# Unit 8 of the third down pass in half-size products, residual rows summed by accumulating transfers, and the first attention's pool reused tile by tile

## The chip, the cores and the metric

The kernel runs on one core of a Trainium2 chip. The metric is device time in microseconds (us) of one launch. One execution is profiled, and all views below are of that execution.

## The reference, cut to what matters

One encoder block over 512 tokens of width 2048, all in fp32: an adaLN modulation, a combined input projection, a global grouped-query attention with normed and rotated q and k, a neighbourhood attention, a gated merge with an output projection and residual, and a SwiGLU feed-forward of inner width 5632 with residual, then a final RMS norm.

```python
qa = apply_rope(rms_norm(qa, q_norm_w[l]), cos, sin)
ka = apply_rope(rms_norm(ka, k_norm_w[l]), cos, sin)
ya = global_gqa(qa, ka, va)
...
merged = sigmoid(ga) * (ya @ w_oa[l]) + sigmoid(gb) * (yb @ w_ob[l])
x = x + g1 * (merged @ w_out[l])
h2 = rms_norm(x, norm2_w[l]) * (1.0 + sc2) + sh2
ff = (silu(h2 @ w_ffn_gate[l]) * (h2 @ w_ffn_up[l])) @ w_ffn_down[l]
x = x + g2 * ff
return rms_norm(x, final_w)
```

## The kernel before, in words

**Products.** An fp32 operand is kept as two tensors of the fast fp32r type, high and low. `split` makes them: ScalarE (ACT) writes the high part (L168), VectorE (DVE) subtracts it for the low part (L170). Each product is three matmuls, high by high, high by low and low by high (`mm3`, L188, L189, L190). Weights stream from HBM through `unit` (L195, SyncE's queue, 512 KB a piece, the tile `raw`) and are split into the tiles `whl`.

**Half-size products.** Many of the large products are done by seven products of half-size blocks in place of eight (a Strassen-Winograd form, indices r = 1 to 7). `wforms` makes the four sums of a weight's blocks (tiles `ta` and `tb`, L696 to L699) and splits them; `sforms` does the same for the activations (four sums of 512 columns, then three splits of 1024 and one of 512 columns). A unit of the down projection done so takes 84 matmuls of 256 columns, a plain unit 96.

**The stages** follow each other: modulation and input projection, the first attention, gates and values, the second attention, the merge and the output projection (which writes the new residual rows x2 to DRAM), gate and up, and then the down projection. Its inner width of 5632 is cut into 11 units of 512 (0 to 10), and the output width into four column groups cc = 0 to 3. The first pass takes units 0 and 1 for all cc, the second pass units 2 to 5, the third pass units 6 to 9, and the last stretch unit 10 with gate2 multiplied into its weights. Each pass loads its sums (`acc<-accd`) and stores them again.

**The third pass** is a loop over cc with `down_group`. For cc = 0 units 8 and 9 come first and plain, then 6 and 7 by half-size products; for cc = 1 to 3, 6 and 7 first and then 8 and 9 plain (`tail`). Behind each unit `late(cc)` issues what is due: at u = 7 the gated sum of the cc before (`gated_sum`: DVE multiplies the sums by gate2 and adds the residual rows `xr`, the result is stored as `x2pd`, and 1 MB of residual rows for the next cc is loaded); behind cc = 1's units 8 and 9 the activations of unit 10 (`fl`); behind cc = 3's unit 7 the load of gate2 over all rows (`gf<-g2d`), which the weights of unit 10 are multiplied by (`gated_split`, L1528); and behind cc = 3's unit 9 the weights of unit 10 and the loads of x2.

**Tiles.** The slots 0 to 2 (`s0...`, `s1...`, `s2...`) hold the activations' forms of units 2 to 4 in the second pass and of units 6 and 7 (slots 0 and 1) in the third; slot 2 holds `xr` and `fl` there. The areas `a0` and `a1` hold the pairs of plain units (`a1` those of unit 8) and later the last weights `w2` and `w3`.

**The first attention.** The pool `p_a` is allocated on the memory that the projection's pool `p_x` leaves. Without `reuse_waits="tile"` the first write to any tile of it waits for all that was done on that memory, with it for the work on that tile's own bytes. Before the attention, 12 tiles of gate sums are stored (`sga<-g_acc`). Then the rotation's table `rp` is loaded (L792, SyncE's queue), and `norm_rope` makes rotated heads on DVE (L811 norm, L812 cosine, L814 sine, L815 sum, tile `rt`), which TensorE transposes (L818, `T<-ident,rt`) among matmuls of the gates' projections.

**What sets the order.** A scheduler places the instructions in each engine's queue; `issue_after`, `behind` and `keep_in_program_order` pin some. Each engine works its queue in order, so an instruction that waits holds all behind it.

Of the kernel before, what the change touches and what calls it, by code (L numbers as in the profile page):

```python
# [20 lines left out]
P = 128  # L21
# [91 lines left out]
def encoder_block(ctx: ExitStack, tc, xp, xT, c, ada1_w, ada2_w, b_ada, norm1_w, w_in, q_norm_w, k_norm_w, bias,  # L113
# [476 lines left out]
    for k1 in range(1, KT + 1):  # L590
# [41 lines left out]
        if k1 < KT:  # L632
            ada1(k1)
    for j in range(12):
        nc.sync.dma_start(sg_a[j], g_acc[j])
# [155 lines left out]
    p_a = tc.alloc_tile_pool(name="p_a", bufs=1, side="right")  # L791
    behind(nc.sync.dma_start(rp, rope.rearrange("p (i s d) -> p i s d", i=NT, s=2)))  # L792
# [372 lines left out]
    x2_d = dram.tile([T, D], F32, name="x2d")  # L1165
# [19 lines left out]
    def residual(cc, g, ssq, eng, x, keep=None):  # L1185
        cs = slice(cc * 512, (cc + 1) * 512)

        def evac(i, b):
# [5 lines left out]
            if keep is not None:  # L1194
                t0 = i // 2 * 256 + i % 2
                nc.sync.dma_start(keep[t0:t0 + 255:2, cs], x(i, cc))
# [187 lines left out]
    def sforms(j, u):  # L1384

        big, low = slots[j]
        e, o = (raw_tile("ffe") for _ in range(2))
        for a, r in enumerate((e, o)):
            nc.gpsimd.dma_start(r, ff_d[u][:, a * 1024:(a + 1) * 1024])
        sa = wq.tile([P, 1024], F32, tag="ta", name="sa", bufs=2)  # L1390
        sb = wq.tile([P, 1024], F32, tag="tb", name="sb", bufs=1)
# [126 lines left out]
    xr = p_e.tile([P, 3072 + 64], F32, tag="s23072", name="xr")  # L1518
    xo = [xr[:, :2048].rearrange("p (i n) -> p i n", i=NT)]
    fl = p_e.tile([P, 4096 + 64], F32R, tag="s24096", name="fl")  # L1520
    wl = {}
    x2p_d = [dram.tile([P, NT, 512], F32, name=f"x2pd{cc}") for cc in range(3)]
# [9 lines left out]
    def late(cc):  # L1532
        def behind(u):
            if cc == 0 and u == 8:
                while bg:
                    pump()
            if cc == 1 and u > 7:
                a = u - 8
                xl_pairs.append(ff_pair(10, a, [fl[:, a * 2048 + e * 1024:a * 2048 + (e + 1) * 1024] for e in range(2)],
                                        pin=tc.keep_in_program_order))  # L1540
            if u == 7 and due:
                due.pop()()
# [4 lines left out]
            if cc == 3 and u == 7:  # L1547
# [3 lines left out]
                rows(wide2[0], g2_d)  # L1551
            if cc == 3 and u == 9:
# [3 lines left out]
                for c in range(3):  # L1556
                    nc.gpsimd.dma_start(x2[c], x2p_d[c])
# [7 lines left out]
    def factor(cc):  # L1565
        return xr[:, 2048 + cc % 2 * 512:2560 + cc % 2 * 512]

    def residual_of(cc):
        nc.gpsimd.dma_start(xo[0], x2_d[:, cc * 512:(cc + 1) * 512].rearrange("(i p) d -> p i d", p=P))
# [105 lines left out]
```

## Time and profile before

| | |
|---|---|
| time of 3 runs | 2459.8, 2462.04 (median), 2468.41 us |
| the profiled execution | 2466.89 us, span 2465.1 us, mean granted clock 0.998 |
| TensorE (PE) busy | 2433.0 us, 99% |
| VectorE (DVE) busy | 2007.1 us, 81% |
| ScalarE (ACT) busy | 1069.2 us, 43% |
| GpSimd (POOL) busy | 150.8 us, 6% |

The span is the time from the first to the last instruction in the trace; the profiled execution's own time is 1.8 us longer. Matmuls overlap in the pipeline, so that a busy TensorE is read by the distance from one matmul's start to the next; an engine's row ends with what ended the idle time ahead of it.

### The profile page before, as it was taken

What the parts mean: (1) busy time and instruction counts of PE and PEld (TensorE: products, weight loads), DVE (VectorE), ACT (ScalarE), POOL (GpSimd) and SP (SyncE); (2) the same over time, 40 slices, a digit from 0 to 9 for tenths busy, and PEclk for the clock granted to TensorE, in tenths of its full rate; (3) what the DMA queues carried; (4) which work ended last, traced back from release to release, by engine and by line L of the source; (5) the groups of instructions that cost most, each with busy time, mean ns of one, the idle gap of its engine ahead of it and who ended that gap; (6) DMA issues with size and microseconds to landing.
All of it is one profiled execution on the core that took longest, in us unless ns stands there. A gap on an engine that the chain in (4) does not pass through costs nothing.

```text
span 2465.1 us, 42367 instructions
## 1 busy us (share of the span) xinstructions
PE 2433.0 (99%) x17327; PEld 2279.4 (92%) x17327; DVE 2007.1 (81%) x2704; ACT 1069.2 (43%) x1466; POOL 150.8 (6%) x255
## 2 busy tenths in 40 slices
PE   8999999999999999999999999999999999999998
PEld 7888888999888888888999999999999998999997
DVE  7995778998677678667899889889899885687877
ACT  5223545544344523337744444444444454433333
POOL 0000000000011111111000000000000000000010
PEclk9999999999999999999999999999999999999999
DMA  9775232455767687867444454444454456546563
GB/s 354 291 261 159 82 98 83 146 180 187 245 206 235 214 297 248 301 204 230 137 154 154 140 163 153 127 156 154 138 171 139 136 189 223 187 155 231 192 246 126
DMA packets 213731, 461.77 MB, mean 187 GB/s; under 512 B 15153, under 2 KB 59553, under 8 KB 204833
## 3 DMA queue, kind: packets, MB, share of 16 engines
q1 hardware_dynamic: 174160, 309.76, 38.6%
q0 software_dynamic: 29872, 132.73, 15.8%
q10 hardware_dynamic: 9504, 16.58, 1.9%
q8 instruction: 136, 2.23, 0.4%
q14 instruction: 59, 0.48, 0.1%
HBM read 412.84 MB, written 46.17 MB: 186 GB/s over the span
## 4 chain that ended last, share of the span: by engine, by line
PE 71%; DVE 14%; issue 8%; DMA 5%; ACT 1%; POOL 0%; DVEq 0%; SPq 0%; POOLq 0%; ACTq 0%
PE mm L190 14%; PE mm L188 14%; PE mm L189 14%; PE S L188 6%; PE S L190 6%; PE S L189 6%; DVE whl L170 3%; PE Y L188 3%; PE Y L189 3%; PE Y L190 2%; DVE raw L524 2%; DMA raw<-in_w_down 2%; PE T L886 1%; DVE g_acc L631 1%; DMA raw<-in_w_in 1%
## 5 line engine op out<-in xcount | busy, mean ns | idle before, releaser
L168 ACT ACTIVATE whl<-raw 128x1024 fp32r<-128x1024 f32 (+1 forms) x483 | 453.7, 943 | 673.9 <-PE mm L190 292.2
L170 DVE TENSOR_TENSOR whl<-raw,whl 128x1024 fp32r<-128x1024 f32 (+1 forms) x483 | 517.5, 1086 | 124.0 <-ACT whl L168 123.7
L168 ACT ACTIVATE whl<-ta 128x1024 fp32r<-128x1024 f32 x124 | 131.4, 1060 | 182.6 <-PE mm L190 112.9
L168 ACT ACTIVATE whl<-tb 128x1024 fp32r<-128x1024 f32 x124 | 131.4, 1060 | 171.7 <-PE S L190 116.5
L170 DVE TENSOR_TENSOR whl<-ta,whl 128x1024 fp32r<-128x1024 f32 x124 | 151.3, 1220 | 41.8 <-ACT whl L168 41.5
L388 DVE SCALAR_TENSOR_TENSOR acc<-mw,cact,acc 128x1024 f32<-128x1024 f32 x124 | 158.8, 1281 | 19.6 <-DMA mw<-in_ada_w 19.3
L170 DVE TENSOR_TENSOR whl<-tb,whl 128x1024 fp32r<-128x1024 f32 x124 | 150.9, 1217 | 5.9 <-ACT whl L168 5.8
L366 POOL DMA_DIRECT2D mw<-in_ada_w x113 | 60.3, 534 | 1357.1 <-DVE acc L388 939.2
L697 DVE TENSOR_TENSOR ta<-raw,ta 128x512 f32<-128x512 f32 x124 | 85.2, 687 | 65.4 <-DMA raw<-in_w_down 27.2
L696 DVE TENSOR_TENSOR ta<-raw 128x512 f32<-128x512 f32 x124 | 85.3, 688 | 36.3 <-DMA raw<-in_w_down 33.8
L188 PE MATMUL mm<-x56h,whl 128*128 128x256 f32 x336 | 92.7, 276 | 0.3 <-DVE c L784 0.2
L189 PE MATMUL mm<-x56l,whl 128*128 128x256 f32 x336 | 92.4, 275 | 0.0
L190 PE MATMUL mm<-x56h,whl 128*128 128x256 f32 x336 | 92.4, 275 | 0.0
L188 PE MATMUL mm<-x3h,whl 128*128 128x256 f32 x320 | 88.1, 275 | 0.5 <-DVE c L782 0.5
L188 PE MATMUL mm<-whl,s 128*128 128x256 f32 x320 | 88.2, 276 | 0.0
L189 PE MATMUL mm<-whl,s 128*128 128x256 f32 x320 | 88.1, 275 | 0.0
L190 PE MATMUL mm<-x3h,whl 128*128 128x256 f32 x320 | 88.0, 275 | 0.0
L190 PE MATMUL mm<-whl,s 128*128 128x256 f32 x320 | 88.0, 275 | 0.0
L189 PE MATMUL mm<-x3l,whl 128*128 128x256 f32 x320 | 88.0, 275 | 0.0
L190 PE MATMUL S<-x56h,whl 128*128 128x256 f32 x320 | 88.0, 275 | 0.0
L188 PE MATMUL S<-x56h,whl 128*128 128x256 f32 x320 | 88.0, 275 | 0.0
L189 PE MATMUL S<-x56l,whl 128*128 128x256 f32 x320 | 88.0, 275 | 0.0
(1879 smaller groups left out, 8909.2 us busy)
## 6 DMA issues: line engine op xcount, KB each, us to landing
raw<-in_w_in SPq DMA_DIRECT2D x133, 512.0 KB, 4.7
mw<-in_ada_w POOLq DMA_DIRECT2D x113, 512.0 KB, 4.5
raw<-in_w_gate SPq DMA_DIRECT2D x92, 512.0 KB, 4.6
raw<-in_w_up SPq DMA_DIRECT2D x88, 512.0 KB, 4.6
raw<-in_w_down SPq DMA_DIRECT2D x88, 512.0 KB, 5.3
raw<-in_ada_w POOLq DMA_DIRECT2D x29, 1024.0 KB, 5.3
raw<-in_w_out SPq DMA_DIRECT2D x48, 512.0 KB, 5.4
ffd<-c SPq DMA_DIRECT2D x10, 1024.0 KB, 4.8
```

The costliest lines, as they stand in the source:

```text
L168: high = pin(S.activation(hi, src, AF.Copy))
L170: latest[:] = [high, pin(eng.tensor_sub(lo, src, hi))]
L188: nc.tensor.matmul(o, lh, rh, start=start, stop=False, **kw)
L189: nc.tensor.matmul(o, lh, rl, start=False, stop=False, **kw)
L190: nc.tensor.matmul(o, ll, rh, start=False, stop=stop, **kw)
L366: mod["queue"].dma_start(w, ada2_w[n * P:(n + 1) * P, :])
L388: behind(V.scalar_tensor_tensor(acc, part, cact[:, k:k + 1], acc, op0=ALU.mult, op1=ALU.add))
L524: V.scalar_tensor_tensor(raw, raw, 1.0, call, op0=ALU.mult, op1=ALU.mult, accum_out=y)
L631: V.tensor_add(acc, acc, b)
L696: V.tensor_sub(t1, b12, b11)
L697: V.tensor_sub(t2_, b22, t1)
L886: nc.tensor.transpose(tp[:, k * P:(k + 1) * P], e[:, k * P:(k + 1) * P], ident)
```

## The change

**First attention.** `p_a` gets `reuse_waits="tile"`, and the load of `rp` is issued behind step k1 = 14 of the projection's loop, ahead of the stores of the gate sums.

**Third pass.** For cc = 1 to 3 unit 8 is done by half-size products, as 6 and 7 (`ss` is 6, 7, 8, the tail 9). Its activations' forms are made during cc = 0: one load of 1 MB (`f8`, in area `a1`, POOL's queue) behind unit 9, then four DVE sums and four splits into slot 2. `xr` goes from slot 2, `fl` to `a1` with its loads on SyncE's queue, `w2` to slot 2, `w3` to `a0`.

**Residual rows.** x2 lies in DRAM as eight tiles of 256 by 512. `gated_sum` only multiplies, and for cc = 0 to 2 a transfer from POOL's queue adds the product to x2 in DRAM (`accum_op=add`). For cc = 3 the residual rows are loaded behind unit 7, the DVE adds them; and cc = 2's gated sum moves from u = 7 to u = 8 in cc = 3.

```diff
@@ -631,6 +631,8 @@
                     V.tensor_add(acc, acc, b)
         if k1 < KT:
             ada1(k1)
+        if k1 == 14:
+            behind(nc.sync.dma_start(rp, rope.rearrange("p (i s d) -> p i s d", i=NT, s=2)))
     for j in range(12):
         nc.sync.dma_start(sg_a[j], g_acc[j])
     p_x.release()
@@ -788,8 +790,7 @@
                 V.tensor_add(d12, p[3], d12)
 
 
-    p_a = tc.alloc_tile_pool(name="p_a", bufs=1, side="right")
-    behind(nc.sync.dma_start(rp, rope.rearrange("p (i s d) -> p i s d", i=NT, s=2)))
+    p_a = tc.alloc_tile_pool(name="p_a", bufs=1, side="right", reuse_waits="tile")
     nw = {}
     for nm, w in (("q", q_norm_w), ("k", k_norm_w)):
         nw[nm] = small.tile([P, HD], F32, tag=f"nw{nm}", name=f"nw{nm}", bufs=1)
@@ -1162,7 +1163,7 @@
     more_buffers(1, 2)
     wq = tc.alloc_tile_pool(name="wq", bufs=1, side="right", reuse_waits="tile")
 
-    x2_d = dram.tile([T, D], F32, name="x2d")
+    x2_d = [[dram.tile([256, 512], F32, name=f"x2d{cc}{t}") for t in range(2)] for cc in range(4)]
     mod["queue"] = nc.sync
     p_r = tc.alloc_tile_pool(name="p_r", bufs=1, side="right", reuse_waits="tile")
     gate = p_r.tile([P, D], F32, name="gate1")
@@ -1192,8 +1193,7 @@
             if ssq:
                 square(x(i, cc), ssq[i][:, cc:cc + 1])
             if keep is not None:
-                t0 = i // 2 * 256 + i % 2
-                nc.sync.dma_start(keep[t0:t0 + 255:2, cs], x(i, cc))
+                nc.sync.dma_start(keep[cc][i // 2][i % 2::2, :], x(i, cc))
         return evac
 
     def w_out_pass(cc, tiles):
@@ -1381,14 +1381,19 @@
                 self.pairs[j] = ff_pair(self.u0 + n, a, place(self.at + n, a, self.off))
             return tuple(Tokens(half(t)[:, :, q]) for t in self.pairs[j])
 
-    def sforms(j, u):
+    def sforms(j, u, room=None):
 
         big, low = slots[j]
-        e, o = (raw_tile("ffe") for _ in range(2))
-        for a, r in enumerate((e, o)):
-            nc.gpsimd.dma_start(r, ff_d[u][:, a * 1024:(a + 1) * 1024])
-        sa = wq.tile([P, 1024], F32, tag="ta", name="sa", bufs=2)
-        sb = wq.tile([P, 1024], F32, tag="tb", name="sb", bufs=1)
+        if room is None:
+            e, o = (raw_tile("ffe") for _ in range(2))
+            for a, r in enumerate((e, o)):
+                nc.gpsimd.dma_start(r, ff_d[u][:, a * 1024:(a + 1) * 1024])
+            sa = wq.tile([P, 1024], F32, tag="ta", name="sa", bufs=2)
+            sb = wq.tile([P, 1024], F32, tag="tb", name="sb", bufs=1)
+        else:
+            e, o, sa, sb = (room[:, n * 1024:(n + 1) * 1024] for n in range(4))
+            nc.gpsimd.dma_start(room[:, :2048], ff_d[u])
+            yield
         a11, a21, a12, a22 = e[:, :512], e[:, 512:], o[:, :512], o[:, 512:]
         V.tensor_add(sa[:, :512], a21, a22)
         V.tensor_sub(sa[:, 512:], sa[:, :512], a11)
@@ -1515,11 +1520,13 @@
         nc.gpsimd.dma_start(acc_d[cc], acc)
 
     f0 = 40
-    xr = p_e.tile([P, 3072 + 64], F32, tag="s23072", name="xr")
-    xo = [xr[:, :2048].rearrange("p (i n) -> p i n", i=NT)]
-    fl = p_e.tile([P, 4096 + 64], F32R, tag="s24096", name="fl")
-    wl = {}
-    x2p_d = [dram.tile([P, NT, 512], F32, name=f"x2pd{cc}") for cc in range(3)]
+    fl, wl = [], {}
+    x2_of = lambda cc, t: x2_d[cc][t].rearrange("(i p) d -> p i d", p=P)
+
+    def load_x2(to, cc):
+        for t in range(2):
+            nc.gpsimd.dma_start(to[:, 2 * t:2 * t + 2], x2_of(cc, t))
+
     sq3 = [small.tile([P, 4], F32, tag=f"sq{i}", name=f"sq3{i}", bufs=1) for i in range(NT)]
 
     def gated_split(k, cc, hi, lo):
@@ -1534,12 +1541,16 @@
             if cc == 0 and u == 8:
                 while bg:
                     pump()
+            if cc == 0 and u == 9:
+                forms = sforms(2, 8, p_s.tile([P, 4096 + 64], F32, tag="a1", name="f8"))
+                next(forms)
+                bg.append(forms)
             if cc == 1 and u > 7:
                 a = u - 8
-                xl_pairs.append(ff_pair(10, a, [fl[:, a * 2048 + e * 1024:a * 2048 + (e + 1) * 1024] for e in range(2)],
-                                        pin=tc.keep_in_program_order))
-            if u == 7 and due:
-                due.pop()()
+                if a == 0:
+                    fl.append(p_s.tile([P, 4096 + 64], F32R, tag="a1", name="fl"))
+                xl_pairs.append(ff_pair(10, a, [fl[0][:, a * 2048 + e * 1024:a * 2048 + (e + 1) * 1024] for e in range(2)],
+                                        nc.sync, pin=tc.keep_in_program_order))
             if cc == 3 and u == 6:
                 xa = p_s.tile([P, 2, NT, 512], F32, tag="s04096", name="xa")
                 xb = p_s.tile([P, NT, 512], F32, tag="s03072", name="xb")
@@ -1549,12 +1560,15 @@
                 gf = p_s.tile([P, 2, D], F32, tag="s14096", name="gf")
                 wide2.extend((gf[:, 0], gf[:, 1]))
                 rows(wide2[0], g2_d)
+                load_x2(x2[3], 3)
+            if u == (8 if cc == 3 else 7) and due:
+                due.pop()()
             if cc == 3 and u == 9:
                 for c in range(2):
                     us = [gated_split(k, c, *wtiles()) for k in range(0, 4, 2)]
                     wl[c] = [tuple(t[:, e * 512:(e + 1) * 512] for t in hl) for hl in us for e in range(2)]
                 for c in range(3):
-                    nc.gpsimd.dma_start(x2[c], x2p_d[c])
+                    load_x2(x2[c], c)
                 nc.scalar.dma_start(wide2[1], final_w.partition_broadcast(P))
         return behind
 
@@ -1562,28 +1576,29 @@
     cl = {8: ahead[8], 9: {a: ff_pair(9, a, place(0, a, 0)) for a in range(2)}}
     due = []
 
-    def factor(cc):
-        return xr[:, 2048 + cc % 2 * 512:2560 + cc % 2 * 512]
-
-    def residual_of(cc):
-        nc.gpsimd.dma_start(xo[0], x2_d[:, cc * 512:(cc + 1) * 512].rearrange("(i p) d -> p i d", p=P))
-        nc.gpsimd.dma_start(factor(cc), g2_d[cc].partition_broadcast(P).rearrange("p o d -> p (o d)"))
+    def factor_of(cc):
+        f = p_e.tile([P, 512], F32, tag="g2f", name="g2f", bufs=2)
+        nc.gpsimd.dma_start(f, g2_d[cc].partition_broadcast(P).rearrange("p o d -> p (o d)"))
+        factors.append(f)
 
     def gated_sum(cc, acc):
-        to = xo[0] if cc < 3 else x2[3]
+        f = factors.pop(0).unsqueeze(1).to_broadcast([P, 2, 512])
         for t in range(2):
             ts = slice(2 * t, 2 * t + 2)
-            behind(V.tensor_mul(acc[:, ts], acc[:, ts], factor(cc).unsqueeze(1).to_broadcast([P, 2, 512])))
-            behind(V.tensor_add(to[:, ts], xo[0][:, ts], acc[:, ts]))
+            behind(V.tensor_mul(acc[:, ts], acc[:, ts], f))
+            if cc == 3:
+                behind(V.tensor_add(x2[3][:, ts], x2[3][:, ts], acc[:, ts]))
+            else:
+                nc.gpsimd.dma_start(x2_of(cc, t), acc[:, ts], accum_op=ALU.add)
         if cc < 3:
-            nc.gpsimd.dma_start(x2p_d[cc], xo[0])
-            residual_of(cc + 1)
-
-    residual_of(0)
+            factor_of(cc + 1)
+
+    factors = []
+    factor_of(0)
     for cc in range(4):
         acc = acc_tile()
         nc.gpsimd.dma_start(acc, acc_d[cc])
-        down_group(cc, (6, 7), cl, acc, late(cc), () if cc else (8, 9), late=cc > 1,
+        down_group(cc, (6, 7, 8) if cc else (6, 7), {9: cl[9]} if cc else cl, acc, late(cc), () if cc else (8, 9), late=cc > 1,
                    after_lead=cc == 1)
         due.append(functools.partial(gated_sum, cc, acc))
     due.pop()()
@@ -1591,7 +1606,7 @@
     g2, fw = wide2
     xs = [tuple(Tokens(half(t)[:, :, q]) for t in xl_pairs[a]) for a in range(2) for q in range(2)]
     for cc in range(2, 4):
-        wt = p_s.tile([P, 4096 + 64], F32R, tag=f"a{3 - cc}", name=f"w{cc}")
+        wt = (p_e if cc == 2 else p_s).tile([P, 4096 + 64], F32R, tag="s24096" if cc == 2 else "a0", name=f"w{cc}")
         hi, lo = (wt[:, 48 + e * 2048:48 + (e + 1) * 2048] for e in range(2))
         for k in range(0, 4, 2):
             sl = slice(k * 512, (k + 2) * 512)
```

The order of instructions on three places follows (a name is out<-in by the program's tiles, then the shape; x2 or x3 is a run of like rows).

**VectorE at the start of the first attention.** Names as above; `st` holds k's projection, `nwk` the norm's weight, `kl` the low part of the transposed k. Before:

```order
L170 TENSOR_TENSOR whl<-raw,whl 128x1024
L811 SCALAR_TENSOR_TENSOR rt<-st,rr,nwk 128x128 x2
L170 TENSOR_TENSOR whl<-raw,whl 128x1024
L812 TENSOR_TENSOR rt<-rt,rp 128x256
L814 TENSOR_TENSOR rt<-rt,rp 128x128 x2
L815 TENSOR_TENSOR rt<-rt 128x256
L811 SCALAR_TENSOR_TENSOR rt<-st,rr,nwk 128x128 x2
L812 TENSOR_TENSOR rt<-rt,rp 128x256
L170 TENSOR_TENSOR kl<-T,kh 128x2x128
```

Of the change (the lines are one further down):

```order
L170 TENSOR_TENSOR whl<-raw,whl 128x1024
L812 SCALAR_TENSOR_TENSOR rt<-st,rr,nwk 128x128 x2
L813 TENSOR_TENSOR rt<-rt,rp 128x256
L815 TENSOR_TENSOR rt<-rt,rp 128x128 x2
L816 TENSOR_TENSOR rt<-rt 128x256
L812 SCALAR_TENSOR_TENSOR rt<-st,rr,nwk 128x128 x2
L813 TENSOR_TENSOR rt<-rt,rp 128x256
L815 TENSOR_TENSOR rt<-rt,rp 128x128 x2
L170 TENSOR_TENSOR kl<-T,kh 128x2x128
```

The weight's split that stood between the norm (L811, now L812) and the cosine (L812, now L813) now stands behind this stretch.

**VectorE in the third pass, cc = 0, from the weight sums of unit 6 on.** `s_21037` and `s_21038` are slot 2's tiles, `f_23713` is `f8`; `whl` are split weights of units 6 and 7. Before:

```order
L697 TENSOR_TENSOR ta<-raw,ta 128x512
L170 TENSOR_TENSOR whl<-tb,whl 128x1024
L698 TENSOR_TENSOR tb<-raw 128x512
L699 TENSOR_TENSOR tb<-raw,ta 128x512
L1468 TENSOR_TENSOR acc<-acc,S 128x2x256
L170 TENSOR_TENSOR whl<-raw,whl 128x512
L170 TENSOR_TENSOR whl<-raw,whl 128x1024
L170 TENSOR_TENSOR whl<-ta,whl 128x1024
```

Of the change:

```order
L699 TENSOR_TENSOR ta<-raw,ta 128x512
L1398 TENSOR_TENSOR f_23713<-f_23713 128x512
L1400 TENSOR_TENSOR f_23713<-f_23713 128x512
L1399 TENSOR_TENSOR f_23713<-f_23713 128x512
L170 TENSOR_TENSOR s_21037<-f_23713,s_21037 128x1024
L170 TENSOR_TENSOR whl<-tb,whl 128x1024
L1401 TENSOR_TENSOR f_23713<-f_23713 128x512
L170 TENSOR_TENSOR s_21037<-f_23713,s_21037 128x512
L700 TENSOR_TENSOR tb<-raw 128x512
L170 TENSOR_TENSOR s_21038<-f_23713,s_21038 128x1024
L1473 TENSOR_TENSOR acc<-acc,S 128x2x256
L701 TENSOR_TENSOR tb<-raw,ta 128x512
```

Unit 8's four sums (L1398 to L1401) and four splits now stand ahead of or among the splits that unit 6 and unit 7 need, three of the sums and one split ahead of `whl<-tb` of unit 6.

**VectorE in the third pass, cc = 3, around unit 9's weights.** The rows `whl<-raw` are unit 9's splits and then unit 10's; L1528 (now L1535) multiplies unit 10's weights by `gf`; the rows of `acc` with `p`, `mm`, `q`, `v` gather the half-size products. Before:

```order
L1577 TENSOR_TENSOR xr<-xr,acc 128x1024
L170 TENSOR_TENSOR whl<-raw,whl 128x1024 x2
L1472 TENSOR_TENSOR acc<-acc,mm 128x2x256
L1473 TENSOR_TENSOR acc<-acc,mm 128x2x256
L1474 TENSOR_TENSOR q<-S,p 128x512
L170 TENSOR_TENSOR whl<-raw,whl 128x1024
L1475 TENSOR_TENSOR acc<-acc,q 128x2x256
L1476 TENSOR_TENSOR v<-S,q 128x512
L170 TENSOR_TENSOR whl<-raw,whl 128x1024
L1479 TENSOR_TENSOR acc<-acc,v 128x2x256
L1480 TENSOR_TENSOR acc<-acc,v 128x2x256
L1528 TENSOR_TENSOR raw<-raw,gf 128x1024 x3
```

Of the change:

```order
L170 TENSOR_TENSOR whl<-tb,whl 128x1024
L1588 TENSOR_TENSOR acc<-acc,g2f 128x1024 x2
L1535 TENSOR_TENSOR raw<-raw,gf 128x1024
L1476 TENSOR_TENSOR acc<-acc,p 128x2x256
L170 TENSOR_TENSOR whl<-raw,whl 128x1024 x3
L1477 TENSOR_TENSOR acc<-acc,mm 128x2x256
L1478 TENSOR_TENSOR acc<-acc,mm 128x2x256
L1479 TENSOR_TENSOR q<-S,p 128x512
L1535 TENSOR_TENSOR raw<-raw,gf 128x1024
L1480 TENSOR_TENSOR acc<-acc,q 128x2x256
L1481 TENSOR_TENSOR v<-S,q 128x512
```

Before, the four splits of `raw` into `whl` (of units 8 and 9) were ahead of the first product with `gf`; now the first product with `gf` is ahead of unit 9's splits.

## Rows read from the trace of the kernel before

**Rows 1.** The page: busy time of each engine, and DMA share in 40 slices.

```profile
PE 2433.0 (99%) x17327; PEld 2279.4 (92%) x17327; DVE 2007.1 (81%) x2704; ACT 1069.2 (43%) x1466; POOL 150.8 (6%) x255
...
DMA  9775232455767687867444454444454456546563
```

**Rows 2.** Timeline of TensorE at the first rotated head (start, duration, line, operation).

```profile
249.83 0.38 PE L188 MATMUL mm<-whl,h3h 128*128 128x512 f32 x1
251.93 0.41 PE L818 MATMUL T<-ident,rt 128*128 128x128 f32 x2 [1.72 <-issue]
```

**Rows 3.** Timeline of VectorE at the same place.

```profile
242.70 1.23 DVE L170 TENSOR_TENSOR whl<-raw,whl 128x1024 fp32r<-128x1024 f32 x1 [0.40 <-ACT whl L168]
246.86 0.61 DVE L811 SCALAR_TENSOR_TENSOR rt<-st,rr,nwk 128x128 f32<-128x128 f32 x2 [2.93 <-DMA sga<-g_acc]
...
250.54 0.42 DVE L812 TENSOR_TENSOR rt<-rt,rp 128x256 f32<-128x256 f32 x1 [1.43 <-DMA rp<-in_rope]
...
251.40 0.42 DVE L815 TENSOR_TENSOR rt<-rt 128x256 f32<-128x256 f32 x1
```

**Rows 4.** Windows: us, then busy PE, PEld, DVE, ACT, POOL; clock, DMA share, GB/s.

```profile
2273.24:2291.99 18.75, 18.75 (x170) 18.75 (x169) 16.88 (x23) 8.17 (x9) 0.53 (x1) 1.00 0.39 127
2291.99:2310.76 18.77, 18.77 (x171) 18.77 (x170) 18.73 (x23) 9.54 (x10) 2.14 (x4) 1.00 0.38 124
2310.76:2332.20 21.44, 21.44 (x195) 21.44 (x194) 15.37 (x20) 4.67 (x5) 0.77 (x1) 1.00 0.80 277
2382.40:2412.61 30.21, 30.21 (x273) 30.21 (x272) 22.90 (x25) 10.07 (x11) 4.99 (x9) 1.00 0.95 361
2228.41:2231.81 3.40, 3.40 (x19) 3.40 (x18) 2.59 (x5) 1.26 (x2) 0.53 (x1) 0.50 0.93 320
```

**Rows 5.** Timeline of VectorE, third pass, cc = 0 and the start of cc = 1.

```profile
2274.58 0.69 DVE L697 TENSOR_TENSOR ta<-raw,ta 128x512 f32<-128x512 f32 x1 [0.62 <-DMA raw<-in_w_down]
2275.19 1.22 DVE L170 TENSOR_TENSOR whl<-tb,whl 128x1024 fp32r<-128x1024 f32 x1
2276.44 0.69 DVE L698 TENSOR_TENSOR tb<-raw 128x512 f32<-128x512 f32 x1
...
2278.25 1.82 DVE L170 TENSOR_TENSOR whl<-raw,whl 128x512 fp32r<-128x512 f32 x2
...
2283.05 0.69 DVE L697 TENSOR_TENSOR ta<-raw,ta 128x512 f32<-128x512 f32 x1 [1.12 <-DMA raw<-in_w_down]
...
2295.59 1.21 DVE L170 TENSOR_TENSOR whl<-tb,whl 128x1024 fp32r<-128x1024 f32 x1
```

**Rows 6.** Timeline of TensorE: first matmul by the split that each needs.

```profile
2279.93 0.28 PE L188 MATMUL T<-whl,s 128*128 128x256 f32 x1
...
2282.61 0.28 PE L188 MATMUL mm<-whl,s 128*128 128x256 f32 x1
...
2283.95 0.28 PE L188 MATMUL mm<-whl,s 128*128 128x256 f32 x1
...
2298.70 0.28 PE L188 MATMUL S<-whl,s 128*128 128x256 f32 x1
```

**Rows 7.** DMA issues of single windows: count, KB each, us from issue to landing.

```profile
acc<-accd POOLq DMA_DIRECT2D x1, 1024.0 KB, 5.1
...
xr<-g2d POOLq DMA_DIRECT2D x1, 256.0 KB, 3.6
...
gf<-g2d POOLq DMA_DIRECT2D x1, 256.0 KB, 9.5
...
raw<-in_w_down SPq DMA_DIRECT2D x1, 512.0 KB, 15.4
```

**Rows 8.** Timeline of GpSimd: the issues of the sums and of gate2.

```profile
2266.27 0.53 POOL L1585 DMA_DIRECT2D acc<-accd  x1 [6.24 <-DMA accd<-acc]
...
2390.40 1.60 POOL L439 DMA_DIRECT2D gf<-g2d  x3 [2.52 <-PE S L190]
```

**Rows 9.** Timeline of VectorE, cc = 3: unit 9's second split, gate2's first product.

```profile
2393.27 1.21 DVE L170 TENSOR_TENSOR whl<-raw,whl 128x1024 fp32r<-128x1024 f32 x1
...
2399.95 2.36 DVE L1528 TENSOR_TENSOR raw<-raw,gf 128x1024 f32<-128x1024 f32 x2 [4.27 <-DMA gf<-g2d]
```

**Rows 10.** Timeline of TensorE, second pass, cc = 3: two waits.

```profile
2226.14 0.38 PE L188 MATMUL S<-whl,s 128*128 128x256 f32 x1 [0.84 <-ACT whl L168]
2227.40 0.38 PE L189 MATMUL S<-whl,s 128*128 128x256 f32 x1 [0.88 <-DVE whl L170]
```

## Prediction

> **What bounds the kernel now.** I read the page first: TensorE is busy for 2433.0 of 2465.1 us, 99%, VectorE for 81%, ScalarE for 43% [rows 1]. So a change can gain in two ways only, by fewer matmuls or by less of TensorE's 32 us without one; and anything else can cost only where it makes TensorE wait. Next I read the windows of the stages that the change touches: in the third pass TensorE's busy time equals the length of each window, there is no wait in it to remove [rows 4]. VectorE is the second: 16.88 of 18.75 us in cc = 0's units 6 and 7, and 18.73 of 18.77 in cc = 1's [rows 4]. That is where work put on VectorE can reach TensorE. Last I read TensorE's timeline at the first rotated head, the one wait that the change aims at [rows 2].
>
> The sum is made against the profiled execution, 2466.89 us. It lies 4.85 us above the median of 2462.04, which is within the scatter of the three runs (2459.8 to 2468.41), so I add the sum to the median. About 0.3%, 7.4 us, is what a measurement of this kernel can tell from no change.
>
> **The first attention: −1.9 us.** TensorE starts a transpose at 251.93, the matmul ahead of it at 249.83 [rows 2]. Matmuls of 256 columns follow each other here by 0.11 us, those of 512 by twice that, so 2.10 − 0.22 = 1.9 us are lost. VectorE's rows say why: the norm could have started at 243.93, where the split ahead ended (242.70 + 1.23), but waited 2.93 us for the stores of gate sums, which read memory that the pool takes over; then the cosine waited 1.43 us for the table [rows 3]. With waits by tile the norm waits for its own tile's bytes only, and the table is issued ahead of those stores. The chain from norm to sum takes 0.61 us and then 1.28 (250.54 to 251.82): ready at about 245.8 in place of 251.8. The order of the change also puts the weight's split behind this chain, so the split that ran at 247.88 runs some 2 us earlier or at the same time; nothing is late. Bounds: 1.7 (the wait as recorded) to 2.1. Nothing would be gained if another transfer still held the tile; no row shows one. The earlier table adds no bytes, it lies ahead of the last weight pieces of the projection, where the DMA engines are busy to five to seven tenths (the page's slices 3 and 4) [rows 1]; if a piece is late by it, it costs a part of the table's 6 us once. I take none.
>
> **Fewer matmuls: −4.0 us.** Two plain units take 21.44 us, two by half-size products 18.75 [rows 4]: 1.345 us for one unit, three times 4.03. The count gives the same: 3 × 12 matmuls at 18.75/168 = 0.112 us are 4.0.
>
> **Unit 8's forms: +3.8 us.** They are four sums of 0.61 us (2274.58 to 2275.19) and three splits of 1.25 (2275.19 to 2276.44) and one of half the columns, 0.61: 6.8 us on VectorE [rows 5], put by the order in front of what unit 6 and 7 still need. I walk through VectorE's rows and ask at each split whether TensorE is there first.
> - Unit 6's `whl<-tb`: ready before at 2276.41, now behind three sums and a split (3.08) at 2279.49; TensorE needs it at 2279.93 [rows 5, 6]. 0.4 us in hand.
> - Unit 7's first split: ready before at 2278.9, now 5.55 later (all four sums, two splits of 1024 and the small one) at 2284.45. TensorE needs it at 2282.61 [rows 5, 6]: 1.8 late.
> - Unit 7's second: before 2280.07, now 6.8 later, 2286.87, against 2283.95: 2.9 late in all.
> - cc = 1, unit 6's `whl<-tb`: before 2296.80. VectorE had only one idle stretch of 1.12 us in between, at 2283.05 [rows 5], so it is 5.7 later, 2302.5, against 2298.70 [rows 6]: 3.8 late in all.
> The lateness counts once, at its largest: 3.8 us. Behind it VectorE has room, since each unit brings it less than TensorE's 9.4 us and the gated sums lose their additions.
>
> This assumes that `f8` has landed by 2275.19. It is issued right behind the load of the sums, 2266.27 + 0.53 [rows 8]. By that row's 5.1 us [rows 7] it lands at 2271.9, in time; if it is served only behind those sums, at 2277.0, then all is 1.8 us later and the term 5.6. Between, I take in time. If the scheduler's order turns out kinder, because VectorE runs further ahead than before, the term is 0: then it needs TensorE's wait of no split at all. Ends: 0 and 5.6.
>
> The Trainium skill's page "DMA: Bandwidth & Descriptors", section Bandwidth, states 6.15 us for 1 MB from HBM, against the row's 5.1; by it `f8` lands at an estimated 2272.9, and the sum would be the same, with a us less in hand.
>
> **Residual rows and the end of the pass: +0.8 us.** An accumulating transfer is not in the trace; its nearest rows are the store and the load of 1 MB that it replaces. It is issued in stretches with a DMA share of 0.38 and 0.80 [rows 4] and nothing waits for it but the reuse of a sums' tile two column groups later. I take 0; the bound is one more 1 MB at the 361 GB/s of the last stretch, 2.9 us of DMA time, which reaches TensorE only if a weight piece is late by it. The activations of unit 10 on SyncE's queue stand among weight pieces of cc = 1, whose loads run several us ahead; 0.
>
> What moves is gate2. It is loaded into a slot that unit 7 frees, so it is issued at unit 7's end in cc = 3, as before, 0.8 us ahead of the last matmul [rows 8]. Before, units 8 and 9's weights had been split ahead of the first product with it [rows 9]. Now unit 9's two splits are queued behind that product on VectorE. Let L be the time from issue to landing: the product starts at unit 7's end − 0.8 + L and takes 1.18 (2.36 for two), a sum 0.6, the first split 1.25; unit 9 needs it a half-size unit later, 9.38 (18.75/2). It is late by L − 7.15. The rows for L: 3.6 us for a 256 KB piece of gate2 in a quiet stretch, 9.5 for this piece in the full stretch (share 0.95), 15.4 for a weight piece there [rows 4, 7]. The change takes two 1 MB loads of x2 away from ahead of this point and puts one behind it, so I take L between 3.6 and 9.5: late by 0 to 2.4, half of the way from 7.15, 0.8 with a part of it for the last weights, whose splits start later.
>
> **Sum:** −1.9 − 4.0 + 3.8 + 0.8 = −1.3. The profiled execution would be 2465.6, and from the median 2460.7.
>
> **The rivals.**
> - *A, the sum*, 2460.7 (50%).
> - *B, VectorE keeps up.* In favour: the rows of cc = 0 show VectorE waiting for weight pieces twice (0.62 and 1.12) [rows 5], so it is ahead of TensorE, and 16.88 of 18.75 leaves 1.87. Against: 6.8 us is more than that. It would give −5.1: 2456.9 (17%).
> - *C, the clock.* TensorE shows two waits of 0.84 and 0.88 us in the second pass [rows 10], and right behind them 3.40 us at a granted clock of 0.50, 1.2 of 2.4 GHz, with 19 matmuls in place of 30 [rows 4]: 11.5 × 0.112 = 1.3 us. The new waits at unit 7 are as long. One such stretch gives 2462.0 (12%). Against it: the wait at the attention, 1.9 us long, is not known to have brought one. The Trainium skill's page "TensorE: Matmul & The Clock Gate", Part 1, says that a gate halves the array's clock when it has been idle and that activity releases it; the trace agrees in the second pass with its 0.50.
> - *D, slower.* gate2's landing decides. Unit 9's splits behind it, with L as the 15.4 us of the weight piece in that stretch: late by 8.2 in place of 0.8, 2468.1. From L = 9.3 on the change is a loss. For it: the row of this very piece is 9.5 now, and x2's load follows on the same queue. Against: that queue has less ahead of it (11%).
> - *E, the two waits of [rows 10] go too* since VectorE's or the transfers' timing shifts: −1.7 − 1.3 more, 2457.7, or with B 2453.9 (7%). Nothing in the diff touches them.
> - *F, the change does not do what it says at the attention*: the transpose waits for something else, +1.9: 2462.6 (3%).
>
> **The numbers.** 2460.7 is A. With B, C, E, F and most of D the range is 2454 to 2468; A alone, by its bounds (0 to 2.4 for gate2, 3.8 to 5.6 for the forms), is 2459.9 to 2464.1. Faster by over 0.3% means below 2454.6: B with E or a run of low scatter, 0.15. Slower by over 0.3% means above 2469.4: D with a bad clock, 0.08. The rest, 0.77, is the same within what can be told.
>
> **What would show it.** Right: no wait at the first transposes; 84 matmuls in unit 8 of cc = 1 to 3 and windows of 28.1 us for three half-size units; new waits of TensorE on VectorE's splits at unit 7 of cc = 0 and unit 6 of cc = 1, 3.8 us in all; unit 9 of cc = 3 starting without a wait or with one under 2.4. Wrong: a wait at unit 9 of over 5 us with gate2's transfer as the releaser on VectorE (D), no waits in the third pass at all (B), stretches of granted clock 0.50 behind the new waits (C).

## The result, and the profile after

The changed kernel takes 2478.01 us (median of 6 runs, 2475.94 to 2480.7) against 2462.12 us for the kernel before, 15.9 us more by the medians; the ratio is 1.0058, 95% interval 1.0047 to 1.0068, which is 14.3 us. A second measurement gave 1.0055 (1.0037 to 1.0073). The forecast was 2460.7, range 2454 to 2468, with a chance of 0.08 for slower. The page says little: TensorE does 36 matmuls fewer and is busy as long, in a longer span of 2475.9 us.

```profile
PE 2434.8 (98%) x17291; PEld 2278.8 (92%) x17291; DVE 2019.8 (82%) x2724; ACT 1078.0 (44%) x1476; POOL 157.5 (6%) x258
```

**The first attention** went as forecast. TensorE's timeline at the first transpose, which was 1.72 us late in [rows 2]:

```profile
246.07 0.38 PE L189 MATMUL mm<-whl,h2h 128*128 128x512 f32 x1
246.29 0.38 PE L819 MATMUL T<-ident,rt 128*128 128x128 f32 x2
```

and VectorE's, where the norm and the cosine of [rows 3] now wait for nothing:

```profile
243.11 0.61 DVE L812 SCALAR_TENSOR_TENSOR rt<-st,rr,nwk 128x128 f32<-128x128 f32 x2
243.75 0.42 DVE L813 TENSOR_TENSOR rt<-rt,rp 128x256 f32<-128x256 f32 x1
```

**The loss** stands in TensorE's waits by line (in all, how many, the longest). Of the first and the fourth, 0.9 and 0.8 us were there before [rows 10], and of the second 0.4; the rest is new, and lies behind 2280 us:

```profile
PE S L189 <- DVE whl L170: 4.0, 5, 1.8
PE mm L189 <- DVE w L170: 3.5, 1, 3.5
...
PE Y L188 <- DVE acc L1490: 1.9, 1, 1.9
PE S L188 <- ACT whl L168: 1.7, 2, 1.0
PE Y L189 <- DVE whl L170: 1.6, 1, 1.6
```

VectorE's timeline at cc = 3's end shows where they begin. The first product with gate2 waits 6.05 us for its transfer, and unit 9's two splits and unit 10's first (the x3) start at 2401.52 behind it. In [rows 9] unit 9's second split had started 6.7 us before that product:

```profile
2391.38 2.35 DVE L1588 TENSOR_TENSOR acc<-acc,g2f 128x1024 f32<-128x1024 f32 x2
2399.78 1.23 DVE L1535 TENSOR_TENSOR raw<-raw,gf 128x1024 f32<-128x1024 f32 x1 [6.05 <-DMA gf<-g2d]
2400.92 0.69 DVE L1476 TENSOR_TENSOR acc<-acc,p 128x512 f32<-128x512 f32 x1
2401.52 3.49 DVE L170 TENSOR_TENSOR whl<-raw,whl 128x1024 fp32r<-128x1024 f32 x3
```

SyncE's timeline shows what else stood behind it. The weight pieces go round a ring of tiles, and a piece is loaded when VectorE has split an older one. In the changed kernel:

```profile
2385.78 1.50 SPq L195 DMA_DIRECT2D raw<-in_w_down  x2
...
2402.77 3.02 SPq L195 DMA_DIRECT2D raw<-in_w_down  x3
```

The products with gate2 that read them tell which these are: unit 10's first two pieces, then its third to fifth. In the kernel before, its second to fifth were issued within 6.7 us:

```profile
2388.15 6.73 SPq L195 DMA_DIRECT2D raw<-in_w_down  x4
```

So from 2386.92, the second of the x2, no weight is asked for during 16 us, and unit 10's third piece, which was issued at 2389.24 before, is issued at 2402.77. Two windows of the changed kernel behind the waits at unit 10 (columns as in [rows 4]) show what TensorE's clock adds: a granted 0.50, 1.2 GHz, in the first, and 0.59 in the mean of the second, whose first matmuls still follow each other at the full clock:

```profile
2422.06:2424.62 2.56, 2.56 (x8) 2.02 (x6) 2.56 (x4) 0.00 (x0) 0.17 (x1) 0.50 0.74 250
2430.68:2434.83 4.15, 4.15 (x12) 3.35 (x12) 3.41 (x4) 1.31 (x4) 0.00 (x0) 0.59 0.02 4
```

### The profile page after: what moved, and what is told of

It is laid out like the page before. It is cut to its first block, busy times and chain, and to the rows that moved or that the text cites. A ratio compares the mean times of both kernels' runs of the same rounds, so it can differ in the third digit from the quotient of the medians.

```text
span 2475.9 us, 42322 instructions
## 1 busy us (share of the span) xinstructions
PE 2434.8 (98%) x17291; PEld 2278.8 (92%) x17291; DVE 2019.8 (82%) x2724; ACT 1078.0 (44%) x1476; POOL 157.5 (6%) x258
## 4 chain that ended last, share of the span: by engine, by line
PE 63%; DVE 20%; DMA 9%; issue 6%; ACT 2%; POOL 0%; DVEq 0%; SPq 0%; ACTq 0%; POOLq 0%
PE mm L190 13%; PE mm L189 13%; PE mm L188 13%; DVE whl L170 6%; PE S L188 5%; PE S L190 5%; PE S L189 5%; DMA raw<-in_w_down 4%; DVE raw L524 2%; PE Y L188 2%; PE Y L189 2%; PE Y L190 2%; DMA raw<-in_w_up 1%; DVE ta L699 1%; DVE tb L700 1%
## 5 line engine op out<-in xcount | busy, mean ns | idle before, releaser
L189 PE MATMUL mm<-whl,s 128*128 128x256 f32 x368 | 101.7, 276 | 1.1 <-DVE whl L170 1.1
L188 PE MATMUL mm<-whl,s 128*128 128x256 f32 x368 | 101.4, 276 | 0.0
L190 PE MATMUL mm<-whl,s 128*128 128x256 f32 x368 | 101.2, 275 | 0.0
```

The lines of the kernel that those rows point to most:

```text
L188: nc.tensor.matmul(o, lh, rh, start=start, stop=False, **kw)
L189: nc.tensor.matmul(o, lh, rl, start=False, stop=False, **kw)
L190: nc.tensor.matmul(o, ll, rh, start=False, stop=stop, **kw)
```

## The experiments

Ratios are to the kernel before on the same chip, with 95% intervals. Kernels that were timed with different runs of the kernel before are compared by their ratios, and a difference in us is then the ratios' difference on 2461.

| kernel | median us | before us | ratio (interval) |
|---|---|---|---|
| attention_only | 2460.16 | 2463.28 | 0.9991 (0.9982 to 1.0000) |
| nine_first | 2469.97 | 2463.28 | 1.0027 (1.0017 to 1.0037) |
| unit8_plain | 2473.03 | 2463.28 | 1.0040 (1.0027 to 1.0052) |
| plain_stores | 2475.60 | 2463.28 | 1.0047 (1.0034 to 1.0060) |
| gate_earlier | 2466.73 | 2460.85 | 1.0022 (1.0013 to 1.0031) |
| unit8_plain_gate_earlier | 2458.65 | 2460.85 | 0.9992 (0.9983 to 1.0000) |
| gate_earlier_plain_stores | 2465.57 | 2460.85 | 1.0020 (1.0011 to 1.0029) |
| gate_earlier_no_sums | 2461.60 | 2460.85 | 1.0004 (0.9996 to 1.0013) |
| sum_behind | 2462.80 | 2461.06 | 1.0003 (0.9995 to 1.0012) |
| forms_behind | 2466.35 | 2461.06 | 1.0017 (1.0008 to 1.0025) |
| change_again | 2475.23 | 2461.06 | 1.0055 (1.0037 to 1.0073) |

**attention_only.** The hunks at `k1 == 14` and at `p_a` of the change, put into the kernel before.

> The attention part alone (waits by tile in its pool, the table loaded ahead), all else as before. Theory 1 (the attention part gains its wait, the loss lies in the third pass): no wait at the first transpose, 1.5 to 2.1 us less, about 2460. Rival (waits by tile let the attention's writes or the early table delay the projection's weights): a new TensorE wait between 170 and 350 us and no gain, 2462 to 2465.

2.2 us less than the kernel before, with an interval that reaches zero, and no wait at the first transposes nor a new one up to 350 us. Theory 1 holds by the waits; the time alone would not settle it.

**nine_first.** In the change, the first products with gate2 are put behind unit 9's last split:

```diff
+            with tc.issue_after(nine[0]):
                 V.tensor_mul(r3, r3, ...)
...
             if cc == 3 and u == 9:
+                nine.append(latest[1].ins)
```

> The change, with unit 9's two splits in cc = 3 ahead of the first product with gate2 on VectorE, nothing else moved by hand. Theory 1 (VectorE stands still on that product for 6.05 us, and behind it stand unit 9's splits, the release of the weight pieces and so unit 10's loads and splits): the wait at unit 9 (1.57) goes, most of the 7 us of waits at unit 10 goes, and with them the two stretches at half clock (3.0): 8 to 11 us less than the change, 2467 to 2470. Rival (unit 8's half-size products hold the weight pieces so long that unit 10's come late in any order): 1.5 to 3 us less, 2475 to 2477, waits at unit 10 as in the change.

7.6 us less than the change (1.0058 to 1.0027), a little under theory 1's 8 to 11 and far from the rival's 1.5 to 3. The wait at unit 9 is gone, and the 16 us in which no weight is asked for are 9. VectorE's timeline shows the splits ahead of the product, which still waits for 2.11 us:

```profile
2394.92 2.36 DVE L170 TENSOR_TENSOR whl<-raw,whl 128x1024 fp32r<-128x1024 f32 x2 [0.27 <-ACT whl L168]
2399.40 1.23 DVE L1538 TENSOR_TENSOR raw<-raw,gf 128x1024 f32<-128x1024 f32 x1 [2.11 <-DMA gf<-g2d]
```

At unit 10 waits of 0.31, 2.07 and 1.47 us stay, and one stretch at half clock. So the order was about half of the loss, not all.

**unit8_plain.** The change without unit 8's forms and with unit 8 plain:

```diff
-        down_group(cc, (6, 7, 8) if cc else (6, 7), {9: cl[9]} if cc else cl, acc, ...
+        down_group(cc, (6, 7), cl, acc, ...
```

> The change with unit 8 plain again in all column groups (no forms, fl and the last weights where they were before); kept are the attention part, the accumulating transfers, the moved gated sum and x2's load. Theory 1 (accumulating transfers are hidden): the attention's gain alone and, at cc = 3's end, waits as before, 2460 to 2462. Rival (the accumulating transfers hold up the queue and the DMA engines): new TensorE waits in the third pass, 2465 to 2470.

By the medians 12.9 us over attention_only, on the same chip. The rival's number is nearer, and part of its mechanism is in the trace: the accumulating transfers hold up the queue. The waits that it expected in the third pass are not there; TensorE waits at unit 10. GpSimd's timeline shows gate2's load at 2396.74, behind the second accumulating transfer, which was itself issued 10.4 us after the first:

```profile
2385.59 1.22 POOL L1588 DMA_DIRECT2D x2d<-acc  x1 [3.53 <-DVE q L1479]
2395.99 1.23 POOL L1588 DMA_DIRECT2D x2d<-acc  x1 [9.19 <-issue]
2396.74 2.18 POOL L439 DMA_DIRECT2D gf<-g2d  x3
```

and VectorE stands still for it longer than in the change:

```profile
2402.88 1.23 DVE L1535 TENSOR_TENSOR raw<-raw,gf 128x1024 f32<-128x1024 f32 x1 [13.36 <-DMA gf<-g2d]
```

**plain_stores.** `accum_op=ALU.add` is taken out of the transfers, so that this kernel leaves the first residual rows out of three quarters of the output.

> The change with plain stores in the place of the accumulating transfers, which leaves the first residual rows out of three quarters of the output. Theory 1: the waits at unit 9 and unit 10 stay, since gate2's landing sets them: 2475 to 2478. Rival (accumulating transfers cost): the sums of the next column group are issued some 6 us earlier, VectorE's late stretch at the start of cc = 3 (1.9 us) goes and gate2 lands earlier: 2468 to 2473.

1.0047 against the change's 1.0058: 2.7 us less, but the intervals overlap. The waits at unit 9 (0.6 in place of 1.6 us) and unit 10 stay, as theory 1 said. The time is unclear, and small. But the rival has one thing right: the wait of 1.93 us for a sum at the start of cc = 3 is gone, in gate_earlier_plain_stores too. VectorE's timeline shows the weight piece ahead of it, for which the changed kernel's VectorE waits 4.52 us:

```profile
2364.88 0.69 DVE L699 TENSOR_TENSOR ta<-raw,ta 128x512 f32<-128x512 f32 x1 [1.41 <-DMA raw<-in_w_down]
```

**gate_earlier.** On nine_first, gate2 goes to the slot that unit 6 frees, x2's rows to unit 7's:

```diff
             if cc == 3 and u == 6:
-                xa = ... tag="s04096"
+                gf = p_s.tile([P, 2, D], F32, tag="s04096", name="gf")
+                wide2.extend((gf[:, 0], gf[:, 1]))
+                rows(wide2[0], g2_d)
             if cc == 3 and u == 7:
-                gf = ... tag="s14096"
+                xa = p_s.tile([P, 2, NT, 512], F32, tag="s14096", name="xa")
```

> The change, with gate2 loaded into the slot that unit 6 frees in cc = 3 in place of unit 7's (x2's rows go to unit 7's), so that it is issued some 9 us earlier, and with unit 9's splits ahead of the first product with it. Theory 1 (VectorE's stand on gate2 and what it delays behind it make the end late): VectorE waits for gate2 nowhere, the waits from unit 9 on fall from 9.2 to under 2 us and the half clock behind them (3.0) goes: 2466 to 2468. Rival (VectorE has no room left at the end of cc = 3 whenever gate2 lands): waits at unit 10 of 4 us or more stay and with them 2470, as with unit 9's splits ahead alone.

8.9 us less than the change, as theory 1 said, and VectorE waits for gate2 nowhere; but one wait of 3.8 us stays at unit 10, where theory 1 had under 2 in all and the rival 4 or more. VectorE's timeline shows it as an order: cc = 3's gated sum stands ahead of the split of `w`.

```profile
2414.49 1.22 DVE L1591 TENSOR_TENSOR acc<-acc,g2f 128x1024 f32<-128x1024 f32 x1
2415.63 1.22 DVE L1538 TENSOR_TENSOR raw<-raw,gf 128x1024 f32<-128x1024 f32 x1
2416.76 1.22 DVE L1593 TENSOR_TENSOR xd<-xd,acc 128x1024 f32<-128x1024 f32 x1
2417.90 1.22 DVE L1591 TENSOR_TENSOR acc<-acc,g2f 128x1024 f32<-128x1024 f32 x1
2419.04 1.22 DVE L170 TENSOR_TENSOR w<-raw,w 128x1024 fp32r<-128x1024 f32 x1
```

TensorE's matmul that needs it:

```profile
2420.31 0.48 PE L189 MATMUL mm<-w,fl 128*128 128x512 f32 x1 [3.79 <-DVE w L170]
```

**unit8_plain_gate_earlier.** The same edit on unit8_plain.

> Unit 8 plain as in unit8_plain, with gate2 loaded into the slot of unit 6 and unit 9's splits ahead of its first product. Theory 1 (the 12.9 us over the attention part alone were gate2's load behind an accumulating transfer on GpSimd's queue): the 13.36 us stand of VectorE goes and with it all waits at unit 10, 2460 to 2462. Rival (the accumulating transfers take DMA time that weights need): waits at unit 10 stay above 3 us, 2465 or more.

By the ratios 11.8 us less than unit8_plain, back at attention_only's ratio, with no wait of TensorE over 0.25 us in the third pass or after it. The accumulating transfers are in this kernel too; what was lost in unit8_plain was the delay of gate2's load.

**gate_earlier_plain_stores.** Both edits.

> As gate_earlier, with plain stores in the place of the accumulating transfers, which leaves the first residual rows out of three quarters of the output. Theory 1 (the accumulating transfers cost 2 to 3 us, by sums that come late and pieces of weights behind them): 2 to 3 us less than gate_earlier. Rival (they are hidden once gate2 is early): within 1 us of it.

1.0020 against 1.0022: the rival holds, plain stores change the time by no more than can be told once gate2 is early.

**gate_earlier_no_sums.** For unit 8, `wforms` splits the raw pieces in the place of `ta` and `tb`, which leaves out the four sums of its weights.

> As gate_earlier, with the four sums of unit 8's weights left out (its products then take the raw blocks, so the output is not the reference's): 7.3 us less work on VectorE over cc = 1 to 3, the same matmuls, splits and loads. Theory 1 (in the third pass three half-size units to a column group leave VectorE too little room): the waits between 2340 and 2380 us, 2.9 us in the two runs with unit 8 in halves so far, fall under 1, about 2 to 3 us less than gate_earlier. Rival (the weight pieces arrive late, held by the ring of tiles): within 1 us of gate_earlier, with the waits as they are.

4.4 us less than gate_earlier, more than theory 1's 2 to 3. The two waits it was to remove (in gate_earlier 0.29 at 2353 and 1.86 at 2373) are not in its trace; the 3.8 us at unit 10 are. Theory 1 holds, with a reserve: with less work VectorE also frees the pieces sooner, so that its own time and the ring's are not told apart.

**sum_behind.** On gate_earlier, the last `due.pop()()` goes behind the last weights:

```diff
-    due.pop()()
...
+    with tc.issue_after(latest[1].ins):
+        due.pop()()
```

> As gate_earlier, with cc = 3's gated sum on VectorE behind the splits of the last weights (w2, w3), where it stood among them. Theory 1 (the 3.8 us wait that gate_earlier keeps at unit 10 is that order, 3.4 us of sums ahead of the split that TensorE needs): the wait falls under 1 us, 3 to 4 us less than gate_earlier, 2462 to 2464. Rival (the last weights' pieces land late): the wait stays, 2466 to 2467.

4.7 us less than gate_earlier, a little more than theory 1's 3 to 4, and no wait over 0.25 us from unit 9 to the end of unit 10's products. Theory 1 holds. This is the kernel before's time (1.0003) with 36 matmuls fewer.

**forms_behind.** On sum_behind, unit 8's forms are pinned behind unit 7's last split in cc = 0.

```diff
+            yield
...
+        with tc.issue_after(latest[1].ins) if room is not None else contextlib.nullcontext():
             V.tensor_add(sa[:, :512], a21, a22)
```

> As sum_behind, with unit 8's forms in cc = 0 behind unit 7's last weight split on VectorE, where they stood ahead of unit 7's first. Theory 1 (VectorE's room in the third pass is used up by the half-size unit 8): the three waits of 2.9 us at units 6 and 7 go, and waits of 1.5 us or more come up in cc = 1 to 3, in all 0 to 1.5 us less than sum_behind. Rival (only the place was bad): 2.5 to 3 us less than sum_behind, with no new wait.

3.4 us more than sum_behind: worse than either theory said. The three waits are gone, and one longer one stands at the start of cc = 1, in TensorE's timeline:

```profile
2286.44 0.28 PE L188 MATMUL S<-whl,s 128*128 128x256 f32 x1
2292.11 0.58 PE L189 MATMUL mm<-whl,s 128*128 128x256 f32 x1 [5.39 <-DVE whl L170]
```

VectorE worked without a pause from 2276.55 to the split that TensorE waited for. Neither of the two places that were tried lets the forms cost nothing.

**change_again and before_again.** The two kernels once more.

> The change once more, on the chip of this job: 14 to 17 us over before, 2474 to 2479, with the same waits as in its first trace: 1.5 to 2 us at unit 9, 7 us or more from unit 10 on, with granted clock 0.50 behind them.

> The kernel before once more, for a second trace. The first one was 4.8 us above the median. If that was the half clock behind the two waits at 2226 us and the wait itself, this trace has less of both and a span near 2460; the wait of 1.7 us at the first transpose stands in it again.

Both much as expected. before_again took 2459.62 us in its one run. Its first transpose waits again, for 1.1 us in place of 1.7, and the two waits of [rows 10] and the half clock of [rows 4] are not in it:

```profile
PE T L818 <- issue: 1.1, 1, 1.1
```

Windows of before_again, the third pass from the first half-size product of cc = 0 to unit 10, and from there to the end:

```profile
2266.20:2405.56 139.36, 139.36 (x1250) 139.36 (x1249) 113.40 (x135) 49.47 (x52) 10.85 (x19) 1.00 0.61 223
2405.56:2457.80 52.24, 42.11 (x206) 36.54 (x204) 41.64 (x80) 16.50 (x43) 0.00 (x0) 0.96 0.23 82
```

The same of change_again:

```profile
2264.34:2407.44 143.10, 137.19 (x1215) 135.86 (x1214) 117.92 (x148) 53.06 (x58) 14.98 (x19) 1.00 0.59 183
2407.44:2472.20 64.76, 47.19 (x206) 39.30 (x204) 47.17 (x84) 20.08 (x47) 2.73 (x3) 0.87 0.33 106
```

3.7 us are lost in the third pass in spite of the fewer matmuls, and 12.5 from unit 10 on. The spans differ by 14.4 us, the medians by 14.2. The first pair of traces differs by 10.8. The two waits near 2225 us are not the reason: the change's first trace holds them too (0.71 and 0.88 us, with half clock behind them). Behind them, up to the end of unit 10's waits, it lost 3.0 us less than change_again.

## Why the prediction was wrong

Sizes below are of change_again against before_again, from start to start of TensorE's matmuls, less the usual distance (for the fewer matmuls, their count times that distance).

| step | forecast | measured |
|---|---|---|
| first attention | −1.9 | −1.3 |
| fewer matmuls | −4.0 | −4.0 |
| unit 8's forms in cc = 0 and 1 | +3.8 | +2.6 |
| end of cc = 2 and start of cc = 3 (room on VectorE) | 0 | +2.7 |
| gate2: unit 9 | +0.8 with the last weights | +1.6 |
| gate2: unit 10 (9.0 less 0.5 before) | in the 0.8 | +8.5 |
| half clock behind the waits | 0 | +3.8 |
| sum | −1.3 | +13.9 (the spans: +14.4) |

**Right:** the attention part, the matmuls, and the forms, whose waits came at the splits that were named, at two thirds of the size. `f8` was in time: it had landed before the first sum.

**The step that failed is "What moves is gate2"**, a term of +0.8 us for which +10.1, and +3.8 of half clock behind it, were measured. Its first half was right and exact: gate2 took 8.8 us to land, so unit 9 should be late by 8.8 − 7.15 = 1.65, and it waited 1.57 us. The failure is the list of what is queued behind the waiting product. I followed unit 9's splits and put the rest into "a part of it for the last weights, whose splits start later". Behind it stood also the gather of the half-size products (now later, since unit 8 is one of them), and with unit 9's splits the release of two tiles of the ring, so SyncE's loads of unit 10's weights from the third piece on, 13 us later than before. At unit 10 TensorE lost five times what it lost at unit 9. nine_first and gate_earlier show it: they move only this product, its load and the slots, shorten the 16 us without a load of weights to 9 and 8, and take 7.6 and 8.9 us off. Some 4 us of unit 10's 8.5 are a second order of the same kind, which gate_earlier keeps: cc = 3's gated sum ahead of the last splits. Moving it, sum_behind took off 4.7 us. It cost little before, 0.35 us of waiting for `w`, since VectorE was not late there. The 0.8 itself does not follow from its bounds either: half of 0 to 2.4 is 1.2.

**The sentence "Behind it VectorE has room" failed too.** A half-size unit brings VectorE less than its 9.4 us, but the gather and the gated sum come on top, and three such units follow each other without a plain unit's pause. At the start of cc = 3 a weight piece came late and the queue behind it held the sum that frees a bank. VectorE's timeline of the changed kernel:

```profile
2366.72 0.69 DVE L699 TENSOR_TENSOR ta<-raw,ta 128x512 f32<-128x512 f32 x1 [4.52 <-DMA raw<-in_w_down]
...
2377.34 0.68 DVE L1490 TENSOR_TENSOR acc<-acc,Y 128x512 f32<-128x512 f32 x1
```

TensorE waited 1.93 us for that sum. gate_earlier_no_sums, with 7.3 us less for VectorE, has no such wait. But the kernels with plain stores have none either, with the same work on VectorE: there the weight piece took 3.6 us from issue to landing in plain_stores, against 6.7 in the changed kernel, where the load of the next sums (`acc<-accd`), held back behind the accumulating transfers, is issued 0.3 us ahead of the piece. So VectorE's work alone does not make this wait, and the zero for the accumulating transfers in the prediction's paragraph on the residual rows is in doubt too. What they cost in time is not shown: those two traces have waits in cc = 2 instead, 1.0 and 1.6 us in all.

**The clock** was rival C, priced for one stretch of 1.3 us; there were two, of 1.6 and 2.2 us, and they came behind the waits of unit 10, not behind those that I named. A wait does not always bring one: behind gate_earlier's 3.79 us, from 2420.31 to 2423.73, the granted clock is 1.00. The two levels and the fall after a wait are those that the Trainium skill's page "TensorE: Matmul & The Clock Gate", Part 1, describes: a gate that halves the array's clock when it has been idle. The changed kernel's trace agrees with 0.50 behind its wait of 1.75 us, and with 0.59 in the mean behind that of 3.52.

**Rival D** had the right place and sign and the wrong reason: it needed a transfer of 15.4 us and priced 8.2 for unit 9. A transfer of 8.8 was enough. Its break-even, a landing time of 9.3 us, was wrong because only unit 9 was counted.

**What half-size unit 8 is worth:** on one chip, gate_earlier takes 8.1 us more than unit8_plain_gate_earlier, and sum_behind's ratio is still 0.0011 above it, 2.7 us, with intervals that just overlap. The 4.0 us of matmuls are not got back in any version run here. The best with the rest of the change is unit8_plain_gate_earlier, 0.9992 (0.9983 to 1.0000), which keeps the attention part and cannot be told from it alone (0.9991). Not settled: how VectorE's time, the ring's tiles and the accumulating transfers share the 2.7 us at the end of cc = 2 and the start of cc = 3, and why some executions of either kernel have the waits near 2225 us and others not.

## What to carry to other kernels

When a change puts a waiting instruction ahead in an engine's queue, price everything behind it until the queue has caught up: what it computes, the buffers it frees and the loads that those buffers hold back. Here the first wait of TensorE was 1.6 us, and 7.6 us came back when the waiting product was put behind the splits. Fewer matmuls gain nothing where the second engine pays for them: count its work over the whole stretch with all that is due there, not for one unit, and load what a product waits for into the slot that comes free first.

## What the hardware showed that was not expected

In each of the three pairs of accumulating transfers of the changed kernel the second is issued 0.3 us after the first has landed. In the pair below no semaphore of the program asks for that: the second depends on VectorE's product alone. GpSimd's timeline of the changed kernel, cc = 1:

```profile
2306.94 1.28 POOL L1592 DMA_DIRECT2D x2d<-acc  x1 [44.58 <-DVE acc L1588]
2313.55 1.22 POOL L1592 DMA_DIRECT2D x2d<-acc  x1 [5.33 <-DVE whl L170]
```

The transfer from issue to landing, with the issue at 2306.94, so that it landed 0.3 us ahead of the second issue:

```profile
x2d<-acc POOLq DMA_DIRECT2D x1, 512.0 KB, 6.3
```

In plain_stores the same two are 1.1 us apart, and the first takes 3.3 us:

```profile
2306.97 0.75 POOL L1592 DMA_DIRECT2D x2d<-acc  x1 [44.69 <-DVE acc L1588]
2308.11 0.75 POOL L1592 DMA_DIRECT2D x2d<-acc  x1 [0.39 <-DVE acc L1588]
```

The changed kernel's other accumulating transfers of 512 KB took 5.8 to 9.1 us. What stands behind the second one on that queue, such as gate2's load in unit8_plain, is held back with it until the first has landed.

This is not shown to be a property of accumulating. Plain transfers on this queue are held in the same way, only later: of four loads of x2 in the changed kernel, 512 KB each, three are issued in a row, and the fourth 0.3 us after the first has landed, which took 6.1 us:

```profile
2382.79 2.15 POOL L1528 DMA_DIRECT2D xa<-x2d  x3 [22.61 <-PE mm L190]
2389.20 0.72 POOL L1528 DMA_DIRECT2D xa<-x2d  x1 [4.26 <-issue]
...
xa<-x2d POOLq DMA_DIRECT2D x1, 512.0 KB, 6.1
```

That the queue has room for a limited amount of work not yet landed, of which an accumulating transfer takes more, would explain both; no run here tests it.
